# Products that nothing reads, issued while the chains of the norms, the first modulation vector and the routing wait

## The chip, the cores and the metric

The kernel runs on one core of one Trainium2 chip. The metric is the device time of one execution in microseconds, the median over several runs. A profile of one execution shows when each instruction ran on TensorE (PE), VectorE (DVE), ScalarE (ACT) and GpSimd (POOL), and when SyncE (SP) issued transfers.

## The reference

Batch 1, 256 tokens, width 1024, everything in float32. Two blocks follow one another, each with two layers.

First block, per layer: a condition vector `c` gives six modulation vectors; then a mixer and a convolutional feed-forward part, each between two norms:

```
mod = silu(c) @ ada_w[layer] + ada_b[layer]
shift_m, scale_m, gate_m, shift_f, scale_f, gate_f = split(mod, 6)
h = rmsnorm(x, mix_pre_g) * (1 + scale_m) + shift_m
x = x + gate_m * rmsnorm(mixer(h), mix_post_g)
h = rmsnorm(x, ffn_pre_g) * (1 + scale_f) + shift_f
x = x + gate_f * rmsnorm(conv_ffn(h), ffn_post_g)
```

The mixer of layer 0 has block-sparse and dilated attention, that of layer 1 latent and stick-breaking attention. The feed-forward part goes 1024 to 5632, a convolution over three tokens, gelu of one half times the other, and 2816 to 1024.

Second block: 16 learned tokens are put in front (272 tokens), and per layer

```
u = rms_norm(h, norm1_g);  h = h + concat(rwkv7, diff_attention, gla)(u @ w_in) @ w_out
u = rms_norm(h, norm2_g)
aff = softmax(u @ router)            # 16 experts
gates, idx = top_k(aff.T, 34)        # each expert takes its 34 best tokens
h = h + scatter(gates * (silu(u[idx] @ w1) * (u[idx] @ w3)) @ w2)
```

with 1408 hidden columns for each of the 16 experts. The output is a last `rms_norm` of the 256 tokens.

## The kernel before, in words

The residual `x` stays in SBUF as 128 partitions x 8 k-tiles x 272 tokens: features on partitions, tokens in the free direction. Weights stream from HBM through a ring of slots, all issued by SP (line 378); a slot is loaded again when TensorE has read it. Most weights of the first block and of the mixers are split into a rounded high part (`whi`, ScalarE, line 401) and a rest (`wlo`, VectorE or GpSimd, line 403), and one product becomes three fast passes (`mm3`). Other products are plain f32 (`mm`, line 388), which the profile shows as two instructions each. The weights of the experts are used as plain f32.

**A norm.** The squares of `x` are multiplied with a block of ones on TensorE (`add_squares`), which gives partial sums per token in a PSUM bank. `token_sums` copies them to SBUF on ScalarE (`g4`) and turns them with small products so that tokens are on partitions. `rstd` scales on VectorE (`rv`, line 450) and takes the power -1/2 on GpSimd (`rr`, line 452). The result is spread over all partitions by transposes (`spread` in the first block, `bcast_tok` in the second, line 440), and then VectorE, ScalarE and GpSimd form the normalised tile in a high and a low part, k-tile by k-tile (`pre_norm`, lines 572 to 578; `norm_split`, lines 1292 to 1294). The products that follow take these k-tiles in order.

**A modulation vector.** `ada(l, third)` is a generator. It loads 4 slots of 2 MB and issues for each of 8 k-blocks the products of the broadcast condition with 4 x 512 columns, into the four row groups of one bank (`adps`); then a copy to SBUF (`adasb`, VectorE, line 507), four transposes (line 440) and an addition (`mod`, line 514). The object `fill` keeps these generators and lays pieces of them between other work; `need` finishes one where its result is wanted. The vector (0, 0) is the first one and is wanted at once.

**The routing.** In `experts` the affinities of all tokens (`aff_s`) are transposed on TensorE, followed by the transposes of `x` (`utok`, `pl`). VectorE then does five rounds of max and match-replace and some scans (the 34 best of each expert, `slT`); TensorE transposes the result, VectorE builds one-hot tiles (`oh`, line 2267), and `gather` multiplies with them to collect the tokens of four experts. Then the experts follow.

**Order.** The order on each engine is planned ahead by a scheduler that takes a priority (`tc.high_priority`) and a model of the times; within the experts, TensorE's order is that of the program text (`manual_schedule`). On the chip each engine takes its instructions in that order. `K.bank()` takes one of 8 PSUM banks, shared by all.

Of the kernel before, what the change touches and what calls it, by code (L numbers as in the profile page):

```python
# [2 lines left out]
L, S, D, KD = 272, 256, 1024, 8  # L3
# [337 lines left out]
class Kit:  # L341
# [111 lines left out]
        return r  # L453


    def add_squares(self, st, k, sq):

        j = 32 * (k % 4)
        self.mm(st[j:j + 32, :sq.shape[1]], self.ones[:, 0:32], sq, start=k < 4, stop=k >= 4)
# [10 lines left out]
def first_block(K, tap):  # L470
# [5 lines left out]
    with ExitStack() as cx:  # L476
# [19 lines left out]
        def ada(l, third):  # L496
            ps = K.bank("adps")
            for kp in range(4):
                w = K.load(A["ada"][l, third, kp])
                for k2 in range(2):  # L500
                    k = 2 * kp + k2
                    for j in range(4):
                        K.mm(ps[32 * j:32 * j + 32], cond[:, k:k + 1].to_broadcast([128, 32]),
                             w[:, k2 * 2048 + j * 512:k2 * 2048 + (j + 1) * 512], start=k == 0, stop=k == 7)
                    yield 1.1
            sb = work.tile([128, 512], F32, name="adasb")
            nc.vector.tensor_copy(sb, ps)
            yield None
            pt = K.bank()
            for b in range(4):  # L510
                K.tr(pt[:, b * 128:(b + 1) * 128], sb[:, b * 128:(b + 1) * 128])
            m = P1.tile([128, 16], F32, name=f"mod{l}{third}")
            o = l * V1["n"] + third * 16
            nc.vector.tensor_tensor(m.rearrange("p (j b) -> p j b", j=4),
                                    pt.rearrange("p (b j r) -> p j b r", b=4, j=4)[:, :, :, 0],
                                    v1[:, o:o + 16].rearrange("p (j b) -> p j b", j=4), op=OP.add)
            MOD[l, third] = m
            yield 0.5
# [23 lines left out]
        def spread(r):  # L542

            bc = K.bank()
            for h in range(2):
                K.tr(bc[:, 128 * h:128 * h + 128], r[:, h:h + 1].to_broadcast([128, 128]), K.ident)
            return bc[:, 0:S]

        def squares():
            return work.tile([128, 2, S], F32, name="sq2", bufs=SQ)  # L550
# [11 lines left out]
        def x_pair(p):  # L562
            return x[:, 2 * p:2 * p + 2, T0:]

        def scale_of(st):

            return spread(K.rstd(K.token_sums(st, (0, 128), squares()[:, 0])[:, 0:2], 2, 1.0 / (32 * D)))

        def pre_norm(hT, bc, gs, sh):
            for k in range(KD):  # L570
# [18 lines left out]
        def post_norm(st, z, last=False):  # L589

            fill(100.0)
            with tc.high_priority(offset=HP1):
                bc = scale_of(st)
                st = K.bank()
                for p in range(4):
                    zs = z[:, 2 * p:2 * p + 2]
                    nc.vector.tensor_tensor(zs, zs, bc[:, None, :].to_broadcast([128, 2, S]), op=OP.mult)
                    (nc.vector if p % 2 == 1 else nc.gpsimd).tensor_tensor(x_pair(p), x_pair(p), zs, op=OP.add)
                    if last:
                        for k in (2 * p, 2 * p + 1):  # L600
                            sq = squares().rearrange("p a b -> p (a b)")[:, :L]
                            square_sums(K, sq, st, k, k)
                    else:
                        pair_sums(st, p, x_pair(p))
            return st
# [533 lines left out]
        for l in range(2):  # L1139
            with ExitStack() as cm:  # L1140
                MP = cm.enter_context(tc.tile_pool(reuse_waits=RW, name="mixp", bufs=1))
                hT = [MP.tile([128, KD, S], F32R, name=f"hT{i}") for i in range(2)]
                oT = [MP.tile([128, KD, S], F32R, name=f"oT{i}") for i in range(2)]
                with ExitStack() as cy:
                    MIXW[0] = cy.enter_context(tc.tile_pool(reuse_waits=RW, name="mixw", bufs=4))
                    K.widen(cy, f"wm{l}", (EXM0, 0)[l])
                    if l == 0:
                        BP = cy.enter_context(tc.tile_pool(reuse_waits=RW, name="bpre", bufs=1))
                        BD = cy.enter_context(tc.tile_pool(reuse_waits=RW, name="bdr", bufs=1, space=bass.MemoryType.DRAM))
                        with tc.tile_pool(reuse_waits=RW, name="bg", bufs=1) as BG:  # L1150
                            bias = bias_table(BP, BG, BD)
                        nc.scalar.dma_start(out=x[:, :, 0:T0], in_=A["metaT"].rearrange("p (k s) -> p k s", k=KD))
                        fill.add(ADA[0, 0])
                    if l == 0:
                        nst = K.bank()
                        fill(4.4)
                        for p in range(4):
                            pair_sums(nst, p, x_pair(p), p % 2 == 1)
                    with tc.high_priority(offset=HP1):
                        bc = scale_of(nst)  # L1160
                    gs_m = gain_scale(l, "mpre", need(l, 0)[:, 8:16], f"gsm{l}")
                    pre_norm(hT, bc, gs_m, MOD[l, 0][:, 0:8])
                    if l == 0:
                        even_mixer(hT, oT, cy, bias)
                    else:
                        C = cy.enter_context(tc.tile_pool(reuse_waits=RW, name="oddc", bufs=1))
                        c1 = C.tile([128, CONST["cst_1"].shape[1]], F32, name="c1")
                        nc.scalar.dma_start(out=c1, in_=A["cst_1"])

                        def c1v(name):  # L1170
                            o, n = C1[name]
                            return c1[:, o:o + n]

                        odd_mixer(hT, oT, cy, c1v)
                    need(l, 1)
                    fill.finish()
                K.widen(cm, f"wo{l}", EXO)
                if EXO:
                    K.turn = 0
                gp = gate_gain(l, "mpost", MOD[l, 1][:, 0:8], f"gpm{l}")  # L1180
                src = A["ab_out" if l == 0 else "cd_out"]
                us = K.units(K.cols(src[0], range(4)) + K.cols(src[1], range(4)))
                fill.add(ADA[l, 2])
                nst = out_proj(us, oT, gp, cm.enter_context(tc.tile_pool(reuse_waits=RW, name="zp", bufs=1)))
            tap(f"xm{l}", x)
            with ExitStack() as cy:
                FP = cy.enter_context(tc.tile_pool(reuse_waits=RW, name="ffp", bufs=1))
                hT = [FP.tile([128, KD, S], F32R, name=f"hF{i}") for i in range(2)]
                if l == 0:
                    fill.add(ADA[1, 0])  # L1190
                with tc.high_priority(offset=HP1):
                    bc = scale_of(nst)
                s2 = need(l, 2)
                gs_f = gain_scale(l, "fpre", s2[:, 0:8], f"gsf{l}")
                gp_f = gate_gain(l, "fpost", s2[:, 8:16], f"gpf{l}")
                pre_norm(hT, bc, gs_f, MOD[l, 1][:, 8:16])
                nst = conv_ffn(l, hT, gp_f, cy)
                if l == 0:
                    fill.add(ADA[1, 1])
            tap(f"xf{l}", x)  # L1200
# [11 lines left out]
def second_block(K, tap, st=None):  # L1212
# [3 lines left out]
    with ExitStack() as c2x:  # L1216
# [41 lines left out]

        def token_scale(st, g4):

            r = K.rstd(K.token_sums(st, (0, 128, 144), g4)[:, 0:3], 3, 1.0 / (32 * D))
            return bcast_tok(lambda t, p: r[p, t:t + 1], 128)

        TT3 = ((0, slice(0, 128), 128, 0), (1, slice(0, 128), 128, 128), (2, slice(96, 128), 32, 240))

        def bcast_tok(col, width):

            b = K.bank()
            for t, r, n, c0 in TT3:
                K.tr(b[:, c0:c0 + n], col(t, r).to_broadcast([n, 128]), K.ident if t < 2 else K.ident[96:128, 96:128])  # L1270
            return b[:, 0:L]
# [913 lines left out]
        def experts(l, ce, uT, swr, st, big, small):  # L2185
# [4 lines left out]
            aff_s = E.tile([128, 3, 16], F32, name="aff")  # L2190
# [3 lines left out]
            with ExitStack() as ct:  # L2194
                X = ct.enter_context(tc.tile_pool(reuse_waits=RW, name="exr", bufs=1))
                st, lt = st
                g4, ls = (X.tile([128, L], F32, name=n) for n in ("g4", "rls"))
                sums = K.token_sums(st, (0, 128, 144), g4)
                for j in range(4):
                    K.mm(sums[32 * j:32 * j + 32, 3:4], g4[:, 240:272], K.ones[:, 0:1], start=False)  # L2200
                r = K.rstd(sums[:, 0:4], 4, 1.0 / (32 * D))
# [28 lines left out]
                for k in range(KD):  # L2230
                    j = 32 * (k % 4)
                    K.tr_mm(pl[j:j + 32, 128 * (k // 4):128 * (k // 4) + 128], x[:, k, 240:272], K.ident)
                nc.scalar.activation(utl, pl[:, 0:256], AF.Copy, scale=r[:, 3:4])
                wk = X.tile([16, L], F32, name="wk")
                t8 = X.tile([16, 8], F32, name="t8")
                for rnd in range(5):
# [137 lines left out]
            with tc.manual_schedule(engines={mybir.EngineType.PE}):  # L2374
# [21 lines left out]
                nst = K.bank("nst")  # L2396
# [60 lines left out]
```

## Time and profile before

| | us |
|---|---|
| time, median of 3 runs | 2673.73 (2670.37 to 2677.88) |
| profiled execution | 2670.22 |
| its span | 2668.5 |
| TensorE busy | 2462.9 (92%) |
| TensorE weight loads | 1502.2 (56%) |
| VectorE busy | 1084.4 (41%) |
| ScalarE busy | 755.4 (28%) |
| GpSimd busy | 207.2 (8%) |

The mean granted clock of TensorE in the profiled execution is 0.948 of the full 2.4 GHz; a row of the page gives it for 40 slices of the span, in tenths. 753 MB are moved. Busy times overlap, and an idle engine that nobody waits for costs nothing. The profile shows the first block up to about 766 us, the mixer of the second block's first layer to about 1046, its experts to about 1710, the second layer's mixer to about 1995 and its experts to about 2658.

### The profile page before, as it was taken

The page shows a single profiled execution, that of the slowest core. Times are in us where ns is not written, and L with a number is a line of the kernel's source. Part 1 is how long each engine was busy: PE and PEld are TensorE (multiplying, and loading weights), DVE is VectorE, ACT ScalarE, POOL GpSimd, SP SyncE. Part 2 cuts the span into 40 slices and gives each one's busy share as a digit, 9 for nine tenths or more (in the row PEclk, how much of TensorE's full clock was granted, in tenths as well). Part 3 has the DMA queues.
Part 4 walks back from the last instruction along what each step waited for, and adds up shares of the span by engine and source line. Part 5 has one row for each costly group of instructions (what it writes and reads, how often), then busy time and mean ns, then how long its engine had stood idle before and what let it go on. Part 6 is the DMA issues. An engine that isn't in the chain of part 4 may idle for free. (4 is left out here: it accounts for less than half of the span.)

```text
span 2668.5 us, 43625 instructions
## 1 busy us (share of the span) xinstructions
PE 2462.9 (92%) x18599; PEld 1502.2 (56%) x18599; DVE 1084.4 (41%) x2308; ACT 755.4 (28%) x1471; POOL 207.2 (8%) x260
## 2 busy tenths in 40 slices
PE   6989999899989998999999898899989999999897
PEld 4769988679978876333323332488774333233222
DVE  3547765567668465121212111384662211111112
ACT  3545545555545252110100000262431101000001
POOL 0011011110023201000000000031110000000000
PEclk8999999999989898999999999798989999999997
DMA  9385443675032325999999999421259999999994
GB/s 366 145 366 221 174 167 127 267 301 190 20 106 73 114 81 229 389 426 424 426 426 424 425 425 425 157 81 55 92 233 372 425 425 424 426 425 425 426 424 166
DMA packets 78194, 753.43 MB, mean 282 GB/s; under 512 B 9600, under 2 KB 13584, under 8 KB 24624
## 3 DMA queue, kind: packets, MB, share of 16 engines
q1 hardware_dynamic: 75072, 748.38, 68.7%
q8 instruction: 146, 2.39, 0.4%
q10 hardware_dynamic: 2928, 2.26, 0.3%
q14 instruction: 48, 0.39, 0.0%
HBM read 749.54 MB, written 1.07 MB: 281 GB/s over the span
## 5 line engine op out<-in xcount | busy, mean ns | idle before, releaser
L388 PE MATMUL bank<-w,mixT 128*34 128x512 f32 (+1 forms) x3072 | 683.2, 578 | 78.1 <-DMA w<-in_ew 78.1
L388 PEld LDWEIGHTS bank<-w,mixT 128*34 128x34 f32 x3072 | 188.3, 115 | 540.0 <-issue 402.9
L403 DVE TENSOR_TENSOR wlo<-w,whi 128x1024 fp32r<-128x1024 f32 (+1 forms) x242 | 298.4, 1235 | 168.9 <-ACT whi L401 167.5
L401 ACT ACTIVATE whi<-w 128x1024 fp32r<-128x1024 f32 x246 | 258.2, 1053 | 318.3 <-PE bank L388 132.8
L388 PE MATMUL bank<-w,hT 128*34 128x512 f32 x1408 | 314.6, 595 | 0.0
L2322 ACT ACTIVATE hid<-bank 34x512 f32<-34x512 f32 (+1 forms) x96 | 53.3, 555 | 763.8 <-PE bank L388 763.8
L388 PE MATMUL up<-hF,whi 128*128 128x256 f32 x1408 | 256.5, 285 | 5.2 <-ACT hF L573 5.2
L2368 DVE TENSOR_TENSOR x<-x,bank 128x272 f32<-128x272 f32 x256 | 95.8, 431 | 326.4 <-PE bank L388 325.3
L388 PEld LDWEIGHTS up<-hF,whi 128*128 128x128 f32 x1408 | 219.4, 191 | 7.0 <-ACT hF L573 6.0
L2323 DVE COPY hid<-bank 34x512 f32<-34x512 f32 (+1 forms) x96 | 62.4, 650 | 378.7 <-ACT hid L2322 377.7
L388 PE MATMUL bank<-u,whi 128*128 128x272 f32 (+1 forms) x896 | 206.3, 323 | 2.5 <-ACT u L1293 2.3
L388 PE MATMUL up<-hF,wlo 128*128 128x256 f32 x704 | 199.2, 284 | 0.0
L388 PEld LDWEIGHTS bank<-w,hT 128*34 128x34 f32 x1408 | 77.8, 112 | 189.2 <-issue 187.3
L388 PEld LDWEIGHTS bank<-u,whi 128*128 128x128 f32 (+1 forms) x896 | 147.4, 198 | 19.1 <-issue 6.6
L388 PE MATMUL bank<-u,wlo 128*128 128x272 f32 (+1 forms) x448 | 135.6, 303 | 4.6 <-DVE wlo L403 3.7
L388 PEld LDWEIGHTS up<-hF,wlo 128*128 128x128 f32 x704 | 134.2, 191 | 0.2
L452 POOL TENSOR_TENSOR rr<-rv,ca 128x3 f32<-128x3 f32 (+4 forms) x28 | 32.7, 1170 | 986.7 <-DVE rv L450 982.3
L2360 DVE COPY ys<-bank 34x512 f32<-34x512 f32 x32 | 22.2, 695 | 196.8 <-ACT ys L2359 196.8
L388 PE MATMUL acc<-gh,wlo 128*128 128x256 f32 x352 | 99.1, 282 | 0.0
L388 PE MATMUL acc<-gh,whi 128*128 128x256 f32 x352 | 99.0, 281 | 0.0
L388 PE MATMUL acc<-gl,whi 128*128 128x256 f32 x352 | 99.0, 281 | 0.0
L388 PE MATMUL bank<-hT,whi 128*128 128x256 f32 (+1 forms) x464 | 88.9, 294 | 7.7 <-ACT hT L573 3.1
(501 smaller groups left out, 3419.7 us busy)
## 6 DMA issues: line engine op xcount, KB each, us to landing
w<-in_ew SPq DMA_DIRECT2D x136, 2048.0 KB, 28.3
w<-in_ew SPq DMA_DIRECT2D x95, 1536.0 KB, 27.1
w<-in_ew SPq DMA_DIRECT2D x112, 1024.0 KB, 28.5
w<-in_ada SPq DMA_DIRECT2D x24, 2048.0 KB, 8.4
w<-in_ffn_up SPq DMA_DIRECT2D x22, 2048.0 KB, 8.4
w<-in_w_in SPq DMA_DIRECT2D x54, 512.0 KB, 3.5
w<-in_ffn_down SPq DMA_DIRECT2D x10, 2048.0 KB, 8.4
w<-in_ab_in SPq DMA_DIRECT2D x5, 2048.0 KB, 15.4
```

What stands on the lines that cost most here:

```text
L388: self.nc.tensor.matmul(out, lhsT, rhs, start=start, stop=stop, skip_group_check=True)
L401: self.nc.scalar.activation(v(hi[:, :n]), src, AF.Copy)
L403: (self.nc.gpsimd if self.splits in self.pool_share else self.nc.vector).tensor_tensor(v(lo[:, :n]), src, v(hi[:, :n].bitcast(F32)), op=OP ...
L452: nc.gpsimd.tensor_tensor(r[:, :n], v[:, :n], self.cst("half")[:, :n], op=OP.pow)
L2322: nc.scalar.activation(hb[0:CAP, :n], pu[0:CAP, :n], AF.Copy)
L2323: nc.vector.tensor_copy(hb[64:64 + CAP, :n], pu[64:64 + CAP, :n])
L2360: nc.vector.tensor_copy(ys[64:64 + CAP], py[64:64 + CAP])
L2368: nc.vector.tensor_tensor(x[:, k], x[:, k], pc[:, :L], op=OP.add)
```

## The change

A helper takes a PSUM bank and issues `n` products of some 128-row tile that lies ready with the first 256 columns of the constants `ca`. Nothing reads the bank. It is called at five places:

```
+    def busy(self, lhsT, n):
+        out = self.bank("busy")
+        for _ in range(n):
+            self.mm(out[:lhsT.shape[1], 0:256], lhsT, self.ca[:, 0:256])
...
 in ada(l, third), after the four products of each k-block:
+                    if (l, third) == (0, 0):
+                        K.busy(w[:, 0:128], 2)
...
 in the first block:
-        def scale_of(st):
-            return spread(K.rstd(K.token_sums(st, (0, 128), squares()[:, 0])[:, 0:2], 2, 1.0 / (32 * D)))
+        def scale_of(st, sums=0, after=0):
+            g4 = squares()[:, 0]
+            out = K.token_sums(st, (0, 128), g4)
+            if sums:
+                K.busy(g4[:, 0:128], sums)
+            r = K.rstd(out[:, 0:2], 2, 1.0 / (32 * D))
+            bc = spread(r)
+            if after:
+                K.busy(r[:, 0:1].to_broadcast([128, 128]), after)
+            return bc
...
 in post_norm:
-                bc = scale_of(st)
+                bc = scale_of(st, 3 * last, 10 * last)
...
 before the mixer and before the feed-forward part, in both layers:
-                        bc = scale_of(nst)
+                        bc = scale_of(nst, 3, 5)
...
 in token_scale of the second block (both mixers and the final norm):
-            r = K.rstd(K.token_sums(st, (0, 128, 144), g4)[:, 0:3], 3, 1.0 / (32 * D))
-            return bcast_tok(lambda t, p: r[p, t:t + 1], 128)
+            out = K.token_sums(st, (0, 128, 144), g4)
+            K.busy(g4[:, 0:128], 3)
+            r = K.rstd(out[:, 0:3], 3, 1.0 / (32 * D))
+            bc = bcast_tok(lambda t, p: r[p, t:t + 1], 128)
+            K.busy(r[:, 0:1].to_broadcast([128, 128]), 4)
+            return bc
...
 in experts, behind the transposes of x and ahead of the selection:
+                K.busy(aff_s.rearrange("p t e -> p (t e)")[:, 0:32], 8)
```

`last` is true for the last norm of the first block alone. In all there are 98 such products: 16 with the first modulation vector, 32 with the four norms ahead of mixers and feed-forward parts, 13 with the last norm of the first block, 21 in the second block's norms and 16 in the two routings.

## Rows read from the trace of the kernel before

**Rows 1.** The page: busy time, share, instructions; granted clock in 40 slices.

```profile
PE 2462.9 (92%) x18599; PEld 1502.2 (56%) x18599; DVE 1084.4 (41%) x2308; ACT 755.4 (28%) x1471; POOL 207.2 (8%) x260
...
PEclk8999999999989898999999999798989999999997
```

**Rows 2.** Timeline, TensorE: start, duration, line, tiles, count [idle before <-releaser].

```profile
461.80 1.03 PE L388 MATMUL bank<-qf,c 128*128 128x256 f32 x4
462.66 0.59 PE L388 MATMUL bank<-qf,ca 128*128 128x256 f32 x2
...
473.34 1.06 PE L388 MATMUL bank<-az,ca 128*128 128x256 f32 x2
474.19 1.06 PE L388 MATMUL bank<-az,c 128*128 128x256 f32 x2
```

**Rows 3.** Timeline, TensorE, first norm and first modulation vector.

```profile
24.26 0.43 PE L440 MATMUL bank<-ca,rr 128*128 128x128 f32 x2 [1.04 <-POOL rr L452]
24.62 7.05 PE L388 MATMUL adps<-w,cond 128*32 128x512 f32 x48
32.48 0.66 PE L440 MATMUL bank<-ca,adasb 128*128 128x128 f32 x4 [0.81 <-DVE adasb L507]
34.66 0.38 PE L388 MATMUL bank<-hT,whi 128*128 128x256 f32 x1 [1.52 <-ACT hT L573]
```

**Rows 4.** Stretches: length; busy by engine (instructions); granted clock; DMA share; GB/s.

```profile
24.60:31.70 7.10, 7.07 (x49) 1.79 (x48) 0.00 (x0) 0.42 (x1) 0.00 (x0) 0.76 1.03 392
34.70:45.60 10.90, 7.54 (x33) 7.05 (x34) 8.48 (x14) 5.18 (x11) 2.69 (x3) 0.53 1.08 410
...
868.00:885.00 17.00, 16.42 (x131) 13.83 (x129) 4.40 (x8) 5.10 (x12) 1.51 (x2) 0.51 0.10 32
...
1080.00:1300.00 220.00, 213.43 (x1094) 74.71 (x1094) 43.62 (x102) 23.22 (x55) 0.00 (x0) 0.98 1.01 423
1690.90:1712.00 21.10, 14.77 (x26) 4.26 (x26) 4.78 (x8) 3.85 (x8) 0.18 (x1) 0.50 0.20 59
```

**Rows 5.** Timeline, norm ahead of the first feed-forward part.

```profile
188.40 0.43 PE L440 MATMUL bank<-ca,rr 128*128 128x128 f32 x2 [1.95 <-POOL rr L452]
188.67 0.72 PE L440 MATMUL bank<-ca,adasb 128*128 128x128 f32 x4
189.43 0.17 DVE L514 TENSOR_TENSOR mod<-bank,v 128x16 f32<-128x16 f32 x1 [1.65 <-PE bank L440]
189.52 1.21 DVE L403 TENSOR_TENSOR wlo<-w,whi 128x1024 fp32r<-128x1024 f32 x1
190.65 0.16 DVE L534 SCALAR_TENSOR_TENSOR gsf<-mod,v 128x8 f32<-128x8 f32 x1
```

**Rows 6.** Timeline, spreads ahead of layer 1's mixer and its feed-forward part.

```profile
397.53 0.69 PE L440 MATMUL bank<-ca,rr 128*128 128x128 f32 x2 [1.04 <-POOL rr L452]
...
557.69 0.69 PE L440 MATMUL bank<-ca,rr 128*128 128x128 f32 x2 [1.95 <-POOL rr L452]
```

**Rows 7.** Timeline, last norm of the first block: square sums behind it.

```profile
762.53 3.61 PE L388 MATMUL bank<-sq,ca 128*32 128x272 f32 x16 [2.59 <-ACT sq L1208]
...
763.74 1.39 ACT L1208 ACTIVATE sq<-x 128x272 f32<-128x272 f32 x4 [0.30 <-POOL x L598]
```

**Rows 8.** Timeline, spreads of the second mixer's norm and of the final one.

```profile
1715.34 0.93 PE L440 MATMUL bank<-ca,rr 128*128 128x128 f32 x3 [1.18 <-POOL rr L452]
...
2661.21 0.93 PE L440 MATMUL bank<-ca,rr 128*128 128x128 f32 x3 [1.18 <-POOL rr L452]
```

**Rows 9.** Timeline, TensorE, first routing: selection, two gathers, first expert.

```profile
1056.38 0.36 PE L440 MATMUL bank<-ca,slT 16*128 16x16 f32 x2 [4.24 <-DVE slT L2255]
...
1057.66 3.97 PE L388 MATMUL bank<-oh,utok 128*128 128x136 f32 x16 [0.73 <-DVE oh L2267]
...
1062.76 2.13 PE L388 MATMUL bank<-oh,utok 128*128 128x136 f32 x16
...
1065.49 4.92 PE L388 MATMUL bank<-w,mixT 128*34 128x512 f32 x22
```

More of the change, by code (lines that the diff above doesn't have):

```diff
@@ L1191, in first_block @@
                 with tc.high_priority(offset=HP1):
-                    bc = scale_of(nst)
+                    bc = scale_of(nst, 3, 5)
                 s2 = need(l, 2)
```

## The prediction, made before the changed kernel ran

> **What bounds the kernel now.** I read the page first, then the timeline of TensorE around each place that the change touches, then a table of stretches for the granted clock. The page shows TensorE busy for 92% of the span, and a clock row that is nearly always at 8 or 9 tenths: little time is left in waits, and little at the low clock [rows 1]. The profiled execution took 2670.22 us (span 2668.5 and 1.7 around it); the median of the runs is 2673.73, so 3.5 us go onto a sum made in the trace. Runs differ by 7.5 us, and about 0.3% (8 us) is what a measurement can tell from no change. Where TensorE is not full there are chains: squares summed, a reciprocal root on GpSimd, a transpose that spreads it, a vector operation. The expert products behind the first experts are bound elsewhere: there the DMA share is 1.01 [rows 4].
>
> **The price of a product.** A product here is two instructions of 256 columns. Four such instructions start in 0.86 us at the full clock and two in 0.85 us at the lower one [rows 2]. So a product costs 0.43 us at 2.4 GHz and 0.85 at 1.2. The change adds 98: 82 of 256 columns onto 128 rows and 16 of 256 columns onto 32, which I price alike. That is 42 us at the full clock. The queue of TensorE is in order, so what lies over a wait is paid by whatever stands behind.
>
> **First modulation vector, with the first norm.** Before: a wait of 1.04 us for the root, the spread at 24.26, then twelve half-blocks of the vector's product without a gap, 24.62 to 31.67, the vector's transposes at 32.48 and the first product of the projection at 34.66 [rows 3]. There is no idle time in those 7.05 us, so nothing hides a product there. The change puts 14 products between blocks ahead of the last one, and the norm's 3 and 5 ahead of or among them; the last 2 lie beside the wait of 0.81 us for the copy. Four of the 14 come before the sums: about +0.5 there, the early products being cold but the squares behind them warm (estimate, half and double of the row prices). The other 18 are 7.7 us. Off this come 1.0 (the wait for the root, filled) and 1.7: the stretch ran at a mean clock of 0.76 [rows 4], and 7.05 × 0.24 = 1.7 is won if it is full throughout. The vector is late by 0.5 + 7.7 - 1.0 - 1.7 = 5.5. Behind it the projection ran at 1.2 GHz from 34.7 to 45.6, with 7.54 us busy and the rest waiting for the normalised tile [rows 4]. At most 7.54 × 0.47 = 3.5 comes back; I take 1.0, because TensorE will again wait there for the vector operations, as it did in the stretch that lost the clock. Net **+4.5**, bounds +2.0 and, with all 18 at the low clock, 18 × 0.85 + 0.5 - 1.0 = +14.8.
>
> **The other three norms of the first block.** In the first feed-forward part the root takes TensorE's wait of 1.95 us; three products (1.28) fit. The spread is at 188.40, the four transposes of the second modulation vector at 188.67, and behind them on VectorE mod, a split (wlo) and gsf, from which the normalised tile comes [rows 5]. The five products stand under the high priority of the norm, the transposes do not: I expect the products ahead, 5 × 0.43 = +2.1 on the transposes. If wlo is moved ahead of the late mod, about 1.1 of it is hidden; if the transposes go first, all. The wait in the mixer of layer 1 is 1.04 (three products overrun it by 0.24), in the second feed-forward part 1.95 [rows 6]. There spread and transposes ran at 1.2 GHz, 0.69 against 0.43 for the same two, so the held clock returns some 0.6 to 0.8 of the 2.1 to 2.4. A part of the rest disappears where wlo fits, in the second feed-forward part: +1.5 and +0.6 (estimates from these rows; bounds 0 and +2.4 each). Warm products of the following projections give nothing: they wait for VectorE, ScalarE and GpSimd. Sum **+4.2**, bounds 0 and +7.
>
> **The last norm and the first norm of the second block.** After the spread TensorE idles 2.59 us and then does 16 square products at 1.2 GHz in 3.61 us, fed by eight squares on ScalarE of which the last four run 763.74 to 765.13 [rows 7]. Ten products (4.3 us) end near 763.8, 1.2 after the first square product could have begun. But at the full clock the 16 need half, and end with ScalarE's last square: 0.75 earlier. The norm behind it then runs warm for another 0.5. Sum **-1.3**, bounds -2 and +1.2.
>
> **The two other norms of the second block.** In mixer 1 and at the end TensorE has been at 1.2 GHz for a long time (0.50 in the stretch before mixer 1) [rows 4], and the wait for the root is 1.18 [rows 8]. Three products at the low price are 2.56: +1.4 on the spread each. Four more behind the spread end within 3.4 us, beside the vector operations. At the end nothing runs behind it to win the time back: +1.4. In mixer 1 the clock may rise earlier: +1.0. Sum **+2.4**, bounds 0 and +3.
>
> **The routing, twice.** TensorE idles 4.24 us while the top-34 chain runs on VectorE. The gather then takes 1057.66 to 1062.76 at 1.2 GHz where the same 24 instructions take 1062.76 to 1065.49 at 2.4 [rows 9], a difference of 2.4. Eight products (3.4 us) fit wholly into the wait. If the clock holds, the first expert starts 2.4 earlier, its slots are free earlier and the DMA stream, which sets the rest, resumes earlier. The second layer's routing repeats it. I take 2.0 each, since the gather still waits a little for its selection tiles: **-4.0**, bounds -4.8 and 0.
>
> The Trainium skill ("TensorE: Matmul & The Clock Gate", section "HAM oscillation — how this bites in real kernels") lays the loss of the clock to idle gaps of TensorE between groups of products. The trace agrees at the routing; between 868 and 885, however, TensorE was busy for 16.42 of 17 us, much of it with products of 32 x 32 and 64 x 64, at a granted clock of 0.51 [rows 4]. By the page alone each filled wait would pay and the routings would give the full -4.8; by the row, 32-column products may fail to hold the clock and give 0.
>
> **The sum.** 4.5 + 4.2 - 1.3 + 2.4 - 4.0 = +5.8; in the profiled execution 2676.0, on the median 2679.5. I say **2679**.
>
> **Rivals.**
> 1. *The clock's falls inside the mixers move* (the other side: faster). Every event behind 770 us is shifted by some microseconds. The stretch 868 to 885 at 0.51 has 17 us at half speed; if the shift lets TensorE keep 2.4 GHz there, 8.4 is won, and as much if layer 1 has such a stretch. It decides from there on: 2679.5 - 16.8 = 2663. For it: TensorE is busy there, so time at the low clock is time lost. Against: no instruction in the stretch is changed.
> 2. *The products stand in front of nothing.* The transposes of the modulation vectors go ahead of the five, and the clock holds through the routings. The norms of the first block then cost nothing (-4.2) and the routings give 0.8 more: 2674.5. For it: the vectors' copies are long done when the spread runs (the wait at 188.40 is for GpSimd alone [rows 5]). Against: the priority.
> 3. *The early products run cold.* The 18 at 14.8 instead of 4.5: 2690. For it: TensorE was at 1.2 GHz for part of 24.6 to 31.7. Against: that stretch was continuously busy and rose; with products ahead of it, it should rise sooner.
> That the products do nothing at all is not possible: they are instructions in the queue.
>
> **How the numbers follow.** My sum, with 2675 to 2684 as its own range, 0.47; rival 1 0.17; rival 2 0.20; rival 3 0.16. Faster by over 0.3% (below 2665.7) is rival 1: 0.17. Slower by over 0.3% (above 2681.8) is rival 3 and 0.14 of the forecast's upper part: 0.30. The rest, 0.53, is within 0.3%. The range runs from 2663 (half of rival 1 outside) to 2688 (most of rival 3 outside).
>
> **What would show it.** Sums of the trace after: transposes of the first vector near 38 instead of 32.5; the modulation transposes of the first feed-forward part 2 us behind the spread, not 0.3; a granted clock of 1.0 through both gathers and the next expert product 2 us sooner, counted from the selection chain's end; the last spread 1.4 later behind its sums. The prediction is wrong if the first vector comes at about its old time (products hidden or reordered), if the gather is again at 0.5, or if the stretches of the mixers between 780 and 1045 take another length than before, since I count them as unchanged.

## The result, and the profile after

The changed kernel is slower: the median of 11 runs is 2695.74 us (2680.94 to 2703.05) against 2676.01 for 11 runs of before (2670.37 to 2677.88). The ratio is 1.0064, 95% interval 1.0046 to 1.0082. A second series gave 1.0071 (1.0046 to 1.0095). The forecast was 2679 with a range from 2663 to 2688: the sign was right, the size about a third of what came, and the time lies outside the range.

The page of after, busy time and granted clock, against [rows 1]:

```profile
PE 2502.4 (93%) x18795; PEld 1526.6 (57%) x18795; DVE 1085.8 (41%) x2308; ACT 755.6 (28%) x1471; POOL 206.2 (8%) x260
...
PEclk9999999999999889999999999798899999999997
```

TensorE is busy for 39.5 us more, about the 42 that 98 products were priced at, and the mean granted clock rose from 0.948 to 0.956. The profiled execution took 2681.52 us with a span of 2679.8: 11.3 more than before. So the first thing to see is that a higher clock and a longer time stand side by side. The second is that this trace holds 11 of the 20 us by which the medians differ; the other 8 are in runs that it does not show. The profiled execution of before, 2670.22, is moreover shorter than each of its 11 timed runs, so the shifts below are against a short one.

Where the 11.3 arise is read by comparing the start of the same instruction in both traces. The shift is +6.8 us at 73 us and stays there to 182; +8.1 behind the first feed-forward part's norm; +10.6 at 422, behind the norm of layer 1's mixer, and +13.1 at 532; +12.9 at 752; +13.1 at 788 behind the first norm of the second block; between +13 and +14.8 in its mixer; from +12.0 to +9.5 across the first routing; +12.1 at 1749, +13.9 at 1915; from +11.1 to +8.9 across the second routing; +10.0 ahead of the final norm and +11.3 at the end.

Timeline of after, TensorE, first norm and first modulation vector, against [rows 3]:

```profile
24.52 1.06 PE L388 MATMUL adps<-w,cond 128*32 128x512 f32 x8
25.52 1.13 PE L388 MATMUL busy<-ca,w 128*128 128x256 f32 x4
26.58 1.07 PE L388 MATMUL bank<-sq,ca 128*32 128x256 f32 x16
28.21 0.60 PE L388 MATMUL bank<-ca,sq 128*128 128x1 f32 x4 [0.56 <-ACT sq L469]
28.68 1.54 PE L388 MATMUL busy<-ca,sq 128*128 128x256 f32 x6
...
39.69 1.13 PE L388 MATMUL busy<-ca,w 128*128 128x256 f32 x4
40.66 0.60 PE L440 MATMUL bank<-ca,adasb 128*128 128x128 f32 x4
44.80 1.22 PE L388 MATMUL bank<-hT,whi 128*128 128x256 f32 x3 [3.55 <-ACT hT L589]
```

Before, the sums of the squares came behind two k-blocks; now four blocks with eight products stand ahead of them. The vector's transposes moved from 32.48 to 40.66, the projection's first product from 34.66 to 44.80. The clock is full from 20.1 to 44.0; it falls in the 3.55 us for which TensorE then waits for the normalised tile.

Timeline of after, norm ahead of the first feed-forward part, against [rows 5]:

```profile
195.16 0.43 PE L440 MATMUL bank<-ca,rr 128*128 128x128 f32 x2 [0.55 <-POOL rr L452]
195.43 2.32 PE L388 MATMUL busy<-ca,rr 128*128 128x256 f32 x10
197.59 0.60 PE L440 MATMUL bank<-ca,adasb 128*128 128x128 f32 x4
198.23 0.17 DVE L522 TENSOR_TENSOR mod<-bank,v 128x16 f32<-128x16 f32 x1 [2.55 <-PE bank L440]
198.44 0.17 DVE L542 SCALAR_TENSOR_TENSOR gsf<-mod,v 128x8 f32<-128x8 f32 x1
```

Three products fill the wait for GpSimd (1.95 before, 0.55 now). The five stand ahead of the modulation transposes, which come 2.43 us behind the spread and not 0.27. VectorE's `wlo` no longer stands between mod and gsf, so 1.4 of it remain. (In the traces below that have no product at this norm, the shift changes here by 0.0 to +1.6.)

Timeline of after, TensorE, first routing, against [rows 9]:

```profile
1063.83 4.00 PE L388 MATMUL busy<-ca,aff 128*32 128x256 f32 x16
1068.35 0.27 PE L440 MATMUL bank<-ca,slT 16*128 16x16 f32 x2 [0.52 <-DVE slT L2276]
...
1069.57 2.09 PE L388 MATMUL bank<-oh,utok 128*128 128x136 f32 x16 [0.72 <-DVE oh L2288]
```

The first gather takes 2.09 us where it took 3.97: behind the products of 32 columns the clock, full from 1064.6, stays so, where it fell at 1056.0 before, and the shift falls by 2.5 here and 2.2 at the second routing.

### The profile page after: what moved, and what is told of

The parts are those of the page before. It is cut to its first block, busy times and chain, and to the rows that moved or that the text cites. A ratio compares the mean times of both kernels' runs of the same rounds, so it can differ in the third digit from the quotient of the medians.

```text
span 2679.8 us, 44024 instructions
## 1 busy us (share of the span) xinstructions
PE 2502.4 (93%) x18795; PEld 1526.6 (57%) x18795; DVE 1085.8 (41%) x2308; ACT 755.6 (28%) x1471; POOL 206.2 (8%) x260
## 5 line engine op out<-in xcount | busy, mean ns | idle before, releaser
L388 PEld LDWEIGHTS bank<-u,whi 128*128 128x128 f32 (+1 forms) x896 | 146.1, 196 | 18.9 <-issue 7.1
```

The costliest lines, as they stand in the source:

```text
L388: self.nc.tensor.matmul(out, lhsT, rhs, start=start, stop=stop, skip_group_check=True)
```

## The experiments

Each kernel is compared with before on the same chip, with medians over 5 to 12 runs; "faster" and "slower" go by the interval of the ratio.

**First group: what the trace does not show.** `all_again` is the changed kernel. The edits of the others take these lines out of it:

```
without_routing:       -  K.busy(aff_s.rearrange("p t e -> p (t e)")[:, 0:32], 8)
only_routing:          only that line is left
without_first_vector:  -  if (l, third) == (0, 0):
                       -      K.busy(w[:, 0:128], 2)
```

> The changed kernel once more, for its own trace and times. Theory P (the products' places): the trace of after shows +11.3 us; the median of its runs is 19.7 above that of before, and its runs lie from 2681 to 2703, those of before from 2670 to 2678. If the extra 8 us and the spread come from how the clock falls in some stretch, a second trace shows a stretch whose shift against before differs from that of the first trace by several us. Theory R (measurement only): the second trace has the same shift, +11 within 2, all along, and the times lie near 2682.

> The changed kernel without the 16 products in the two routings. Theory P: the routings returned 2.5 and 2.2 us in the trace of after (shift 11.97 to 9.48 and 11.07 to 8.91), so this is 4.6 us slower than the changed kernel, about +24 against before in the median. Theory S: the extra time and the spread of the changed kernel come from the experts behind a routing whose clock was held; then this kernel is not slower but faster than the changed one, by up to 9 us, and its runs spread by less than 10 us.

> Of the change only the 16 products in the two routings. Theory P: faster than before by 4.6 us (0.17%), each gather at a granted clock of 1.0. Theory S: the runs spread by 10 us or more, and the median is slower than before by 5 us or more.

> The changed kernel without the 16 products between the k-blocks of the first modulation vector; those of the norm behind it stay. Theory P: the first vector comes 16 x 0.43 = 6.8 us earlier than in the changed kernel or nearly, so the time is 5 to 6.8 us below the changed kernel's. Rival: the eight products of the first norm hold the vector as well, and only 3.5 us return.

| kernel | ratio to before, 95% interval | median us | lowest to highest |
|---|---|---|---|
| all_again | 1.0071 (1.0046 to 1.0095) | 2697.93 | 2684.97 to 2716.09 |
| without_routing | 1.0115 (1.0098 to 1.0133) | 2709.58 | 2704.73 to 2711.62 |
| only_routing | 0.9999 (0.9983 to 1.0014) | 2677.43 | 2668.51 to 2686.27 |
| without_first_vector | 1.0009 (0.9991 to 1.0028) | 2679.84 | 2672.57 to 2694.65 |

The second trace of the changed kernel has a span of 2697.7, 18 us more than the first. Its shift against before agrees with that of the first within 1.5 us up to 1738 us (+12.0 there, the first has +12.1); at 1798 it is +25.4. These 13 us arise in the mixer of the second layer alone, and 4 more behind them in the same mixer (+28.6 at 1990, the first has +11.1). The other three traces of this group have the same step there: +12.0 from 1738 to 1798 in without_routing and in only_routing, +13.1 in without_first_vector. The stretch in only_routing (columns as in [rows 4]):

```profile
1756.90:1787.50 30.60, 30.60 (x130) 24.98 (x130) 16.63 (x33) 11.91 (x30) 6.23 (x11) 0.50 0.12 35
```

and in the first trace of the changed kernel:

```profile
1760.90:1764.40 3.50, 3.50 (x18) 3.50 (x17) 2.47 (x7) 1.89 (x5) 2.59 (x4) 0.51 0.48 150
1764.40:1824.00 59.60, 57.89 (x1031) 48.94 (x1030) 50.19 (x100) 33.08 (x72) 18.17 (x23) 1.00 0.22 67
```

In the one TensorE works for 30.6 us without a gap at half speed; in the other the clock is low for 3.5 us and then full. I call them the long and the short stretch. only_routing shows that none of the added products is needed near it: the program of that mixer is the one of before.

What follows: theory R falls (two traces of one kernel differ by 18 us, 13 of them at one place). Theory S falls too: without the routings' products the kernel is not faster but slower by 12 us, and its five runs all lie high. The gain in the routings is there in each of these traces that has the products (2.2 to 2.5 us each); in without_routing the shift rises at the first one, by 1.8, as it does in the second trace of before (below), so the products are worth more than the one trace of before showed, and theory P's +24 was short of the +32 measured. But in the time of only_routing nothing is left of it, 0.9999, and its own trace shows one reason: -2.2 us at the first routing, +12.0 in the second mixer, -2.4 at the second routing. Without the first vector's products the kernel gives back 18 us in the median, more than their 6.8; its runs fall into six between 2672 and 2676 and six between 2684 and 2695.

**Second group: the long stretch, and two parts alone.** The cause of the stretch was sought where its clock falls. TensorE waits for a `wlo` of VectorE there, 1.96 us in only_routing. The edit puts four products ahead of that wait, in the second layer's mixer only. In all four kernels that have them the planner also put a few VectorE and ScalarE instructions 5 to 15 us behind that wait in another order; what this does by itself was not run.

```
 in chains, behind the five products of KB with AR:
+    if (l, hp, d, hh) == (1, 1, 0, 0):
+        K.busy(K.ident, 4)
```

`changed_and_mixer_fill` has it beside the whole change, `routing_and_mixer_fill` beside the routings' products alone. `only_first_vector` keeps of the change `K.busy(w[:, 0:128], 2)` in `ada`, `only_four_norms` keeps `scale_of(nst, 3, 5)`.

> The changed kernel with 4 more such products in the second layer's mixer, behind the first group of AR x KB products, ahead of TensorE's wait for wlo. Theory L (a long stretch at the low clock in that mixer sets the extra time: 30 to 34 us at 0.5 in four of the traces, 3.4 in the other two, 13 us between them): the wait is filled, the stretch is short in every run, and the times lie within 8 us of each other at 2682 to 2688, the median 10 us below the changed kernel's. Rival: the clock is lost there for another reason than this wait, and the times keep two groups 13 us apart.

> Of the change only the 16 products in the routings, and the 4 products in the second layer's mixer. Theory L: before and the routing-only kernel have the long stretch in some of their runs too (2678 to 2687); with the wait filled they keep the others, 2668 to 2674, so the median is 4 to 8 us below before. Rival: no change against the routing-only kernel, 2677.

> Of the change only the 16 products between the k-blocks of the first modulation vector. Theory P: 14 of them stand ahead of the vector's last block and nothing hides them, so in the trace everything behind 60 us is 6 to 7 us later, and that stays to the end. Rival: products that keep the clock up let the blocks run faster and the shift is 3 or less.

> Of the change only the 3 and 5 products at the four norms ahead of mixers and feed-forward parts. Theory P: at the first norm about nothing (without the vector's products the shift at 60 us was 0.0), +1.8 at the first feed-forward part, +1.6 at the second mixer, +0.5 behind it, so +4 to +5 at 760 us. Rival: the modulation transposes are not held up and the sum stays under 2.

| kernel | ratio to before, 95% interval | median us | lowest to highest |
|---|---|---|---|
| changed_and_mixer_fill | 1.0025 (1.0006 to 1.0045) | 2687.61 | 2677.42 to 2693.81 |
| routing_and_mixer_fill | 0.9978 (0.9961 to 0.9996) | 2674.00 | 2666.92 to 2677.86 |
| only_first_vector | 1.0032 (1.0012 to 1.0052) | 2686.82 | 2680.64 to 2698.65 |
| only_four_norms | 1.0013 (0.9992 to 1.0035) | 2683.55 | 2674.40 to 2695.01 |

Before had 2679.56 on this chip, so ratios are to be read, not microseconds. Four products that do nothing take the changed kernel from 1.0064 and 1.0071 to 1.0025, some 11 us, as theory L said; with the routings' products alone they give a kernel that is faster than before and than the changed one. No trace with them has the long stretch. In changed_and_mixer_fill the shift also falls by 4.8 us further on in that mixer, where a second stretch at half speed lasts 6.8 us (17.0 in the first trace of the changed kernel), so a part of the 11 us can lie there. Theory L was wrong in one point: the runs were to lie within 8 us, and they span 16; other stretches differ from run to run too. In only_first_vector the shift is +6.0 at 77 us, as expected, but it does not stay: it grows to +21.1 at the end, in parts whose program is that of before (+3.1 in layer 1's attention, +4.0 between the second block's mixers, +3.2 late in the second one, +2.7 behind it). The profiled run took 2691.32 with the short stretch. In only_four_norms the shift goes by -1.6 at the first norm (only_routing, which has no products there, has -1.7), +1.8 at the first feed-forward part, +1.6 at the second mixer, +3.3 through layer 1's attention, where no product was added, and 0 at the second feed-forward part; at 767 us it is +4.8, as expected, but by luck: the +3.3, of which the second trace of before has +2.1, was no term of that sum, and the traces without products at the first feed-forward part reach +1.6 there. The second block's second mixer then adds 13.2.

**Third group: which part brings the long stretch.** The edits take out or leave the two calls in `token_scale`, or the last norm's `scale_of(st, 3 * last, 10 * last)`; `only_mixer_fill` is before with the four products of the second group.

> The changed kernel without the 3 and 4 products of the second block's norms (both mixers and the end). Sum of the places as the traces show them: the final norm gives back 1.4 us, the first mixer's norm about 0.5, the second's 1.3, so 3 us below the changed kernel. Theory M (TensorE that comes warm into the second mixer reaches the wait for wlo more often, and with it the long stretch at the low clock): 8 to 12 us below the changed kernel, and fewer than half of the runs in the upper group.

> Of the change only the 3 and 4 products of the second block's norms. By the places: +3 us against before. Theory M: +8 or more in the median, with two groups 13 us apart. The spread of the final norm is 1.4 us later behind its sums in either case.

> Of the change only the 3 and 10 products of the first block's last norm. My prediction had -1.3 for it; the trace of after showed +0.2 between 765 and 788 us. Products by the places: 0, within 1 us, in the trace at 765; the median within 0.2% of before.

> The kernel before with nothing of the change but 4 products in the second layer's mixer, ahead of TensorE's wait for wlo. Theory L: before meets the long stretch in a part of its runs, so the median falls by 3 to 5 us and the highest times by 10. Rival: nothing (the gain with the routing's products was the routing's): within 0.1%.

| kernel | ratio to before, 95% interval | median us | lowest to highest |
|---|---|---|---|
| without_second_block_norms | 1.0050 (1.0031 to 1.0069) | 2693.59 | 2684.53 to 2702.80 |
| only_second_block_norms | 1.0041 (1.0023 to 1.0058) | 2691.03 | 2679.92 to 2695.68 |
| only_last_norm | 1.0000 (0.9984 to 1.0016) | 2678.05 | 2673.17 to 2689.43 |
| only_mixer_fill | 0.9989 (0.9973 to 1.0004) | 2674.20 | 2665.72 to 2684.34 |

The second block's norms alone cost 11 us where their places give 3. Seven of their ten runs lie between 2690 and 2696, three between 2680 and 2682; of before, 3 of 33 on this chip lie above 2686. That is theory M's picture. But the changed kernel without them keeps 1.0050, 4 to 6 us lower where theory M had 8 to 12, and half of its runs are high: these norms are one way to the long stretch, not the only one. The last norm is worth nothing that can be told from no change. For `only_mixer_fill` the interval touches 1: before loses little to the stretch.

**Fourth group: the second mixer's norm.** `only_second_mixers_norm` makes the 3 and 4 products at that norm alone; `before_again` is before, for a second trace.

> The kernel before, unchanged, for a second trace. Its one trace had the short stretch in the second layer's mixer, and its time (2670) is the lowest of all its runs. If the stretch is a matter of when TensorE's gaps come, this trace either has the short one and a time below 2680, or the long one (30 us or more at 0.5) and a time above 2682; a long stretch with a time of 2677 would say that the stretch isn't what parts the runs.

> Only the products of the second block's norms, with the 4 products ahead of the wait for wlo in the second layer's mixer. Without the 4 products: +0.41%, seven of ten runs in an upper group above 2690. Theory L: the upper group goes, the median is +3 us against before (the final norm's 1.4, the mixers' 1.5) or, as the 4 products also help before by 3, +0. Rival: these norms cost 8 to 11 us for a reason of their own and it stays at +0.3% or more.

> Only the 3 and 4 products at the norm of the second layer's mixer. If it is these that bring TensorE to the wait for wlo in another moment, more than half of the runs lie in an upper group 13 us over the lower one, which is at +1.3 (2677 to 2680). If the share is that of before (3 of 33 above 2686), the median is +1 us and the share comes from shifts further ahead.

| kernel | ratio to before, 95% interval | median us | lowest to highest |
|---|---|---|---|
| before_again | 0.9998 (0.9988 to 1.0009) | 2674.76 | 2670.79 to 2679.93 |
| second_block_norms_and_mixer_fill | 1.0007 (0.9993 to 1.0020) | 2676.09 | 2666.72 to 2681.93 |
| only_second_mixers_norm | 1.0043 (1.0028 to 1.0057) | 2685.97 | 2682.65 to 2689.94 |

Seven products at one norm cost as much (0.43%) as all of the second block's norms (0.41%), and with four products some 35 us behind them these norms are at 1.0007. The six runs with the seven products lie between 2682 and 2690, and not in the two groups that were expected. Against the second trace of before, the trace of this kernel is 10.2 us longer: +12.0 in the long stretch, +1.3 at the norm, -3.1 elsewhere. The traces show how. Timeline of before_again, TensorE, the second mixer; the low stretch lies inside it:

```profile
1754.68 1.18 PE L388 MATMUL bank<-low,sw 64*128 64x272 f32 x4
...
1757.42 0.39 PE L388 MATMUL bank<-u,wlo 128*128 128x272 f32 x1 [0.73 <-DVE wlo L403]
...
1759.59 0.66 PE L388 MATMUL bank<-u,whi 128*128 128x272 f32 x2
...
1762.57 1.38 PE L388 MATMUL bank<-AR,KB 64*128 64x128 f32 x10
1763.88 0.52 PE L388 MATMUL bank<-u,whi 128*128 128x272 f32 x2
1764.64 0.39 PE L388 MATMUL bank<-u,wlo 128*128 128x272 f32 x1 [0.24 <-DVE wlo L403]
```

The same part of only_second_mixers_norm:

```profile
1753.02 1.18 PE L388 MATMUL bank<-low,sw 64*128 64x272 f32 x4
...
1755.76 0.39 PE L388 MATMUL bank<-u,wlo 128*128 128x272 f32 x1 [0.74 <-DVE wlo L403]
...
1758.17 0.41 PE L388 MATMUL bank<-u,whi 128*128 128x272 f32 x2
...
1759.39 1.38 PE L388 MATMUL bank<-AR,KB 64*128 64x128 f32 x10
1760.70 0.52 PE L388 MATMUL bank<-u,whi 128*128 128x272 f32 x2
1763.19 0.39 PE L388 MATMUL bank<-u,wlo 128*128 128x272 f32 x1 [1.97 <-DVE wlo L403]
...
1768.33 2.50 PE L388 MATMUL bank<-AR,KB 64*128 64x128 f32 x10
```

And of second_block_norms_and_mixer_fill, with the stretch table of the 100 us around it:

```profile
1754.57 0.39 PE L388 MATMUL bank<-u,wlo 128*128 128x272 f32 x1 [0.73 <-DVE wlo L403]
...
1758.20 1.38 PE L388 MATMUL bank<-AR,KB 64*128 64x128 f32 x10
1759.51 1.99 PE L388 MATMUL busy<-ca 128*128 128x256 f32 x8
...
1762.01 0.39 PE L388 MATMUL bank<-u,wlo 128*128 128x272 f32 x1 [0.25 <-DVE wlo L403]
```

```profile
1723.30:1825.00 101.70, 96.57 (x1344) 83.63 (x1344) 78.63 (x155) 54.42 (x113) 28.83 (x35) 1.00 0.24 75
```

In all three the wait of 0.73 comes first. In before_again the clock falls behind it; the products that follow take 0.66 for 0.41, TensorE issues the last pair ahead of the second `wlo` 6.46 us behind the first, not 4.94, and that wait shrinks to 0.24, because VectorE, which makes the `wlo`, is not slowed (it starts it 8.7 and 8.9 us behind the `low` product shown). The clock returns and stays, as in the first trace of the changed kernel. In only_second_mixers_norm the clock holds through the first wait; TensorE arrives early, waits 1.97, and then the clock falls, ahead of products of 64 rows (2.50 for 1.38) and of 64 x 64. There it stays low though TensorE is never idle:

```profile
1765.40:1796.20 30.80, 30.80 (x132) 25.40 (x132) 17.34 (x35) 12.61 (x31) 6.32 (x11) 0.50 0.11 35
```

Timeline of the same kernel at the norm itself, against [rows 8]:

```profile
1720.49 2.91 PE L388 MATMUL busy<-ca,mixT 128*128 128x256 f32 x6
1723.19 0.88 PE L440 MATMUL bank<-ca,rr 128*128 128x128 f32 x3
1723.99 2.21 PE L388 MATMUL busy<-ca,rr 128*128 128x256 f32 x8
1725.85 0.60 PE L388 MATMUL bank<-u,whi 128*128 128x272 f32 x2
```

The clock rises at 1724.4, among the products behind the spread: 23.5 us ahead of that mixer's first `low` product (5.1 us ahead of the one shown), in the two traces of before 18.5 and 18.6 us ahead. That is what the products bought, at +1.3 us for the place; the clock is lost again 41 us later.

The stretch is short in 4 of the 13 traces without the four products: both of before, the first of the changed kernel and only_first_vector. There the clock falls 8.4 to 8.8 us behind that `low` product. It is long in the nine others, where it falls 14.3 to 17.5 us behind it, after a second wait of 1.96 or 1.97 us. In the four traces with the four products it is short twice and absent twice. What parts the traces is when the clock rose: in the six short ones 18.5 to 18.9 or 21.9 to 22.1 us ahead of that `low` product, in the eleven others 17.3 to 17.7 or 22.6 to 23.7. The earlier times are those of the kernels with products at this norm, so each kind of kernel has both outcomes; the two with the four products that are among the eleven have no fall where the nine have the long stretch. before_again went as expected: the short stretch, and 2679.69 for the profiled run.

The long stretch is not the only part that moves by itself. The two traces of before, both with the short one, differ by 9.5 us: 5.1 in the first layer's mixer of the second block and 3.5 between it and the second mixer. The first of these, in before and in before_again (columns as in [rows 4]):

```profile
788.00:1040.00 252.00, 238.73 (x3390) 202.05 (x3388) 160.23 (x378) 107.60 (x252) 51.61 (x64) 0.93 0.28 102
788.80:1045.90 257.10, 243.85 (x3390) 206.38 (x3388) 160.68 (x378) 107.40 (x252) 51.16 (x64) 0.90 0.28 99
```

The same instructions take 249.2 to 257.5 us there in the 17 traces.

## Why the prediction was wrong

**The step that failed** is the term for the second mixer's norm. "In mixer 1 the clock may rise earlier: +1.0": the clock did rise earlier, and the place cost +1.3, so far right. But the term was closed there, with the mixers' stretches between 780 and 1045, and by silence those of the second layer, counted as unchanged. What the runs showed in its place: that norm alone costs 0.43% (0.28 to 0.57), 11.5 us on 2675; in its trace 12.0 arise in the stretch 41 us behind it. Nor was the first layer's mixer unchanged: the two traces of before alone have 252.0 and 257.1 us there.

**Rival 1** named the thing, clock falls inside the mixers that move, and gave it the wrong sign: it asked which stretch could be won and not which one before had escaped. The wait behind which the clock is lost in the nine traces with the long stretch, 1.96 or 1.97 us in them, stands in the timeline of before:

```profile
1755.18 0.39 PE L388 MATMUL bank<-u,wlo 128*128 128x272 f32 x1 [0.23 <-DVE wlo L403]
```

It could be read as a wait that a faster TensorE lengthens; the prediction left it out, as nothing was changed there. What rival 1 did foresee came small: in the first trace of the changed kernel the stretch that was at 868 lasts 13.6 us at half speed and not 17.0, which gives 1.6 back.

**Rivals 2 and 3** did not occur: the five products stand ahead of the modulation transposes, and the clock is full from 20.1 us on, behind the first two products.

**The first modulation vector** was mis-sized: +4.5 forecast; +6.8 and +8.0 at the end of the first projections in the two traces of the changed kernel, +6.0 alone, 0.32% (0.12 to 0.52) in the time. (Traces without these products have -2.1 to +0.3 there.) The vector's own lateness was the wrong part: its transposes came 8.2 us later, and not 5.5. A reason is in the rows: a k-block with its two products takes 2.06 us at the full clock (24.52 to 26.58), where the prices of the sum make it 1.75 (0.86, and 7.05 x 0.76 / 6 = 0.89 for the block), and there are eight such pairs. That eight products and not four came ahead of the squares, since the planner moved two k-blocks up, was not foreseen either. The projection gave back 1.4 of the 8.2, where 1.0 was forecast.

**The other norms of the first block**: 4.2 forecast. In the trace of after the first feed-forward part gave +1.4, the second mixer's norm +2.5, the second feed-forward part -0.2: 3.7, near the forecast, though the places without products change by up to 1.6 as well. The further +2.5 in layer 1's attention up to 532 is no price of the products, for the second trace of before has +2.1 there. The products did stand ahead of the modulation transposes, and `wlo` did move, as the text allowed. Alone they cost 0.13% (-0.08 to 0.35).

**The last norm**: -1.3 forecast, +0.2 between 752 and 788 us measured, 1.0000 alone. The square products did not end 0.75 us earlier, because ScalarE's last four squares came later. They wait for products of the first four, which now stand behind the ten (772.41 to 776.83); before, the wait there was 0.30, for GpSimd [rows 7]. Timeline of after:

```profile
777.57 1.39 ACT L1224 ACTIVATE sq<-x 128x272 f32<-128x272 f32 x4 [1.49 <-PE bank L388]
```

**The final norm**: +1.4 forecast; +1.3 measured (+10.0 to +11.3).

**The routings**: -4.0 forecast, -2.5 and -2.2 measured. Products of 32 columns did hold the clock. In the median this is hidden by the long stretch; with that filled, the kernel with the routings' products is at 0.9978 and the one without at 0.9989, whose intervals overlap.

The places of the change thus sum to +8.6 in a trace with the short stretch, where 5.8 was forecast; the other 2.7 of its 11.3 us arise between them. What the median has beyond that is put down to the long stretch: taken by the gap in the times, 12 of 20 runs of the changed kernel lie above 2695, against the 2681 to 2691 of the others, and their granted clock is lower, 0.946 to 0.954 against 0.956 to 0.960. For the single runs this is not shown, as only one of the 12 has a trace, and only_first_vector reached 2691.32 without the long stretch.

Not settled is how often a kernel meets the long stretch, and why. Kernels with other parts of the change alone have it too (the four norms, the last norm, the routings), though their second mixer is instruction by instruction the one of before; both traces of before have the short one. All that the traces show is that there a microsecond in the time at which the clock rises goes with one outcome or the other.

The Trainium skill ("TensorE: Matmul & The Clock Gate", section "Why this matters for your kernels") advises against idle gaps of TensorE between bursts of products, but speaks of longer ones than the 1.97 us behind which the clock fell here. What came then, 30.8 us at half speed with no gap at all, no such gap explains. For the same reason the prediction's "by the page alone each filled wait would pay" goes beyond the page: apart from the routing's 4.24 us, the waits that it lists are 2.59 us or shorter.

## What to carry to other kernels

Filling a wait with products pays where a measured stretch behind it runs at the low clock and nothing stands in the queue behind the filler, as at the routing; it costs most of its price, or all of it, where another dependent operation does (the modulation transposes), or where TensorE was not waiting at all (the first vector). A faster TensorE arrives earlier at every later wait on another engine: list the short waits behind the place, and ask which become long and what kind of products follow them. Where single runs of one kernel differ by more than the effect, compare two traces of the same kernel, the one before the change too, before explaining one.

## What the runs showed that I had not expected

Four products that nothing reads, 1.99 us in the trace, in a wait of 1.97, change the time of the changed kernel, 2.7 ms, by some 11 us; that of before they change by 3, which is not clear of noise. A stretch of 30 us without an idle moment ran at half speed; the same instructions run at full speed in the other traces. The best kernel of the study is not the changed one but before with the 16 products of the routings and those 4: 0.9978 (0.9961 to 0.9996) of before.
